# Hybrid SSD, attention and S5 trunk: the scan tables' powers, computed block by block among attention and the first output product

## The chip, the cores and the metric

The kernel runs on one core of one Trainium2 chip. The metric is the device time of one execution in microseconds; the median of the runs is compared. The engines are TensorE (PE in the profile; its weight loads are PEld), VectorE (DVE), ScalarE (ACT), GpSimd (POOL) and SyncE (SP), which issues most of the loads. DMAs are also issued by POOL.

## What is computed

A decoder trunk with two layers on 256 positions of width 2048, in float32. Layer 0 feeds one input projection to an SSD mixer and to causal attention, and maps both back by one output projection. Layer 1 is a diagonal complex state-space mixer (S5) with a gated product behind it. Cut to what matters here:

```python
def reference(x, ...):
    # layer 0
    z, xbc, dt, q, k, v, gate = split(x @ in0_w)
    xs, B, C = split(silu(causal_depthwise_conv(xbc)))
    y_a = rms_norm((ssd_scan(xs, dt, B, C) + d * xs) * silu(z))
    y_b = attention(rotary(q), rotary(k), v) * silu(gate)
    x = layer_norm(alpha * x + concat(y_a, y_b) @ out0_w)
    # layer 1
    u, gate = split(x @ in1_w)
    lam_bar = exp(lam * dt)                       # 128 groups x 64 complex states
    h_t = lam_bar * h_{t-1} + B_bar @ u_t         # per group of 16 channels
    y = gelu(Re(C @ h_t) + d * u)
    ga, gb = split(y @ glu_w)
    x = layer_norm(alpha * x + ((ga * sigmoid(gb)) * silu(gate)) @ out1_w)
```

## The kernel before

**Products.** All large products are done in float32 through pairs of a high and a low part. A unit of work is 256 rows by 512 columns of a weight: SP loads it (`raw`, L221), ScalarE takes the high part (`wh`, L224), VectorE the low part (`wl`, L226), and TensorE runs three matmuls for each tile (L277 with the weight as the stationary operand, L264 with the activation). Weights are split three units ahead, in rings of four buffers. A product has 8 units (16 in the first output product), and the products follow one another without a pause: two for B and C, four for the convolved x, four for z, then for each of four groups of heads q, k, v and gate, then four output products of 16 units, and then layer 1.

**Side work.** Everything else is written as small jobs which are put between the units. `jobs` holds the jobs that must be done within the next product; `pump` takes them evenly over its units. `back` holds slower work that is spread over many units, up to a unit given by `goal`. The order in which instructions stand on each engine is not the written order: a planner simulates the engines with costs of its own, and on each engine puts next what is ready by its own due times, the earliest written first. It fixes that order before the run. Each engine then works through its queue in order.

**The S5 tables.** `trig_job` and `table_job` compute `phi` (a complex number of modulus 1 for each of 64 columns), `rho` and others from the parameters, on VectorE and ScalarE, while the first convolved product runs. From these come the tables of sixteen blocks, which go to memory as `wb[b]` (128 x 1792) and are loaded in layer 1 (`load`, the tile `wt`):

- `phasor_job` computes, on POOL, the powers 0 to 63 of `phi` by doubling, cosines and sines in `cs`, with the products in `pq`: two memsets (L603, L604), two copies (L606), then six steps of two multiplies (L611), a subtraction (L613) and an addition (L614), and the DMAs to columns 1280 to 1791 of `wb` (L617). One job serves two blocks, on 8 columns of `phi`. `cs` and `pq` lie in the big buffer F behind `cbm`, whose place the attention output takes later. Two such jobs are put into `jobs` behind each of the four convolved products.
- `block_jobs(b)` computes the rest of block b: `bars` and `efs` on VectorE (`bb`, `et`, `tm`, and `ob`, which L663 begins), `pes` with transposes on TensorE and a copy on ScalarE (L678) and the store of `ob` on POOL (L685), and for each second block `mts` with the store of `om` (L698). `ob` has two buffers. These jobs go into `back` within the first group of heads, with a goal at the end of the third output product.

**The scan's sum of squares.** The SSD scan runs as `head_jobs` out of `back`, from the first z product to the first v product. For each two of its sixteen steps `comb` squares a result on ScalarE (L779) into a tile of the tag `c2` (three buffers of 2 KB a partition), and POOL adds it to `ssq` (L781).

**Other work on POOL.** The rotary add of q and k (L832) for every group of heads. Once layer 0 is written, its pools of buffers are released, and the rows of the layer norm are loaded by SP into that memory (L977).

The functions that the diff touches:

Of the kernel before, what the change touches and what calls it, by code (L numbers as in the profile page):

```python
# [12 lines left out]
OP = mybir.AluOpType  # L13
# [3 lines left out]
P = 128  # L17
# [141 lines left out]
def trunk(tc, io, out):  # L159
    nc = tc.nc  # L160
    V, A, G, T = nc.vector, nc.scalar, nc.gpsimd, nc.tensor
    count = [0]

    def nm(s):
        count[0] += 1
        return f"{s}_{count[0]}"

    with ExitStack() as top:
# [23 lines left out]
        def big(tag, shape, dt=F32):  # L192
            return slot.tile(shape, dt, tag=tag, name=nm(tag))
# [36 lines left out]
        jobs = deque()  # L230
        back = deque()
# [18 lines left out]
        def finish():  # L250
            while back:
                back.popleft()()
            goal[1] = 0.0
# [27 lines left out]
        def product(kind, hl, nu=CU, prelude=None):  # L281
            ps = banks()
            for u in range(nu):
                if prelude:
                    prelude(u)
                split_to(unit[0] + 3)
                wpair = ready.pop(unit[0])
                if kind == "w":
                    wmm(ps, u, nu, hl, wpair)
                else:  # L290
                    last = u == nu - 1
                    steps = [(j, o) for o in range(2) for j in range(UK)] if last else [(j, o) for j in range(UK) for o in range(2)]
                    for j, o in steps:
                        xmm(ps, o, wpair, j, hl(u * UK + j), u == 0 and j == 0, last and j == UK - 1)
                unit[0] += 1
                pump(nu - 1 - u)
            return ps
# [55 lines left out]
        wb = [dram.tile([P, 1792], F32, name=f"wb{b}") for b in range(16)]  # L353
# [9 lines left out]
        with ExitStack() as l0:  # L363
# [3 lines left out]
            def a4(shape, dt=F32):  # L367
                return wk.tile(shape, dt, tag="a4", bufs=6, name=nm("a4"))
# [4 lines left out]
            def c2(shape):  # L373
                return wk.tile(shape, F32, tag="c2", bufs=3, name=nm("c2"))
# [130 lines left out]
            conv_jobs(ps, 4, cT)  # L505
            fmem = big("F", [P, 4096])
            cbm = fmem[:, 0:1536].rearrange("p (g n) -> p g n", g=4)
            cs = fmem[:, 1536:2560].rearrange("p (a q c) -> p a q c", a=2, q=8)
            pq = fmem[:, 2560:3584].rearrange("p (i a q c) -> p i a q c", i=2, a=2, q=8)

            def cb_job(g):
                def go():
                    px = aux()
                    T.matmul(px[:, 0:256], bT[:, g, 0:P], cT[:, g, :], start=True, stop=True)
                    T.matmul(px[:, 256:384], bT[:, g, P:S], cT[:, g, P:S], start=True, stop=True)
                    V.tensor_tensor(cbm[:, g, 0:128], px[:, 0:128], C("tril"), op=OP.mult)
                    A.activation(cbm[:, g, 128:256], px[:, 128:256], AF.Copy)
                    V.tensor_tensor(cbm[:, g, 256:384], px[:, 256:384], C("tril"), op=OP.mult)
                return go
# [77 lines left out]
                        V.tensor_tensor(tq, ai, br, op=OP.mult)  # L597
                        V.tensor_tensor(w[:, 1, :, k], tp, tq, op=OP.add)

            def phasor_job(k):  # L600
                def go():
                    sl = slice(8 * k, 8 * k + 8)
                    G.memset(cs[:, 0, :, 0:1], 1.0)  # L603
                    G.memset(cs[:, 1, :, 0:1], 0.0)  # L604
                    for i in range(2):
                        G.tensor_copy(cs[:, i, :, 1], phi[:, i, sl])  # L606
                    n = 1
                    while n < 64:
                        m = min(n, 63 - n)
                        for i in range(2):  # L610
                            G.tensor_tensor(pq[:, i, :, :, 0:m], cs[:, :, :, 1 : m + 1],  # L611
                                            cs[:, i, :, n : n + 1].unsqueeze(1).to_broadcast([P, 2, 8, m]), op=OP.mult)
                        G.tensor_tensor(cs[:, 0, :, n + 1 : n + 1 + m], pq[:, 0, 0, :, 0:m], pq[:, 1, 1, :, 0:m], op=OP.subtract)  # L613
                        G.tensor_tensor(cs[:, 1, :, n + 1 : n + 1 + m], pq[:, 0, 1, :, 0:m], pq[:, 1, 0, :, 0:m], op=OP.add)  # L614
                        n *= 2
                    for i in range(2):
                        nc.gpsimd.dma_start(wb[2 * k + i][:, 1280:1792].rearrange("p (a n) -> p a n", a=2),  # L617
                                            cs[:, :, 4 * i : 4 * i + 4, :].rearrange("p a q c -> p a (q c)"))
                return go

            ktp = [None]
# [85 lines left out]
            def xs_jobs(ps, j):  # L707
                xT = a4([P, 4, S])
                conv_jobs(ps, 8 + 4 * j, xT)

                def back(t):
                    def go():
                        px = aux()
                        transpose4(px, [xT[:, f, t * P : t * P + P] for f in range(4)])
                        A.activation(xs[:, t, 512 * j : 512 * j + 512], px, AF.Copy)
                    return go

                while held:
                    jobs.append(held.popleft())
                held.extend([back(0), back(1)])  # L720

            for j in range(4):
                ps = product("w", xhl)
                xs_jobs(ps, j)
                jobs.extend([phasor_job(2 * j), phasor_job(2 * j + 1)])

            sz = big("D", [P, KT, S])
            ssq = wk.tile([P, S], F32, name="ssq")
# [73 lines left out]
            def scale_job(f):  # L802
                def go():
                    for ft in (f, f + 1):
                        V.scalar_tensor_tensor(sz[:, ft, :], sz[:, ft, :], PR("normg")[:, ft : ft + 1], ssq, op0=OP.mult, op1=OP.mult)
                return go
# [15 lines left out]
            def rope_jobs(ps, dst):  # L822
                def rot(i):
                    def go():
                        pv = ps[i].rearrange("p (f n) -> p f n", n=S)
                        q = dst[:, 2 * i : 2 * i + 2, :]
                        tm = b3([64, 2, S])
                        A.activation(q[64:128], pv[64:128], AF.Copy)
                        V.tensor_tensor(q[0:64], pv[0:64], cosb, op=OP.mult)
                        V.tensor_tensor(tm[0:32], pv[32:64], sinb[32:64], op=OP.mult)  # L830
                        V.tensor_tensor(tm[32:64], pv[0:32], sinb[0:32], op=OP.mult)
                        G.tensor_tensor(q[0:64], q[0:64], tm, op=OP.add)  # L832
                    return go

                jobs.extend([rot(0), rot(1)])
# [61 lines left out]
            for g in range(4):  # L897
                ps = product("w", xhl)
                qT = a4([P, 4, S])
                rope_jobs(ps, qT)  # L900
                ps = product("w", xhl)
                kT = a4([P, 4, S])
                rope_jobs(ps, kT)
                ps = product("x", xhl)
                v = a4([P, 2, 512])
                jobs.extend([lambda ps=ps, v=v, t=t: A.activation(v[:, t, :], ps[t], AF.Copy) for t in range(2)])
                if g == 0:
                    finish()
                    back.append(rms_job)
                    back.extend([scale_job(2 * f) for f in range(8)])  # L910
                    for b in range(16):
                        back.extend(block_jobs(b))
                    goal[0] = unit[0] + 13 * CU + 6 * CU
                ps = product("w", xhl)
                sg = a4([P, 4, S])
                jobs.extend([lambda ps=ps, sg=sg, i=i: A.activation(sg[:, 2 * i : 2 * i + 2, :].rearrange("p f n -> p (f n)"), ps[i], AF.Silu)
                             for i in range(2)])
                attn_jobs(g, qT, kT, v, sg)
# [364 lines left out]
```

## Time and profile before

| | us |
|---|---|
| median of 3 runs (1377.31 to 1377.97) | 1377.62 |
| the profiled execution, whole | 1377.72 |
| its span in the profile | 1375.6 |
| TensorE busy | 1356.2 |
| VectorE busy | 981.8 |
| ScalarE busy | 679.5 |
| POOL busy | 306.2 |

A row of a group of instructions reads: line, engine, operation, written tile <- read tiles with the shape, count | busy us, mean ns of one | idle time of the engine just before them and what ended it. In a row of the timeline the first number is the start, the second the length, and a bracket gives the idle time before it and the releaser. A row of the waits gives the total, the number and the longest. Stretches give the busy time of the engines, then TensorE's granted clock, the DMA share and GB/s.

### The profile page before, as it was taken

Reading aid. Unit: us, or ns where it says so; the run is one execution under the profiler, and the core shown is the slowest. Engines: PE = TensorE matmul, PEld = TensorE weight load, DVE = VectorE, ACT = ScalarE, POOL = GpSimd, SP = SyncE. Lnnn points to the kernel's source line nnn. Section 1 sums busy time; section 2 is a strip of 40 time slices with the busy share of each in tenths; the row PEclk is TensorE's granted clock in tenths of the full one; section 3 lists DMA queues with packets and bytes.
Section 4 is the critical chain, followed back from the end, with each engine's and each line's share of the span. In section 5 each row is a group of like instructions: output and inputs, shape, how many; then the busy total and the mean of one; then the engine's idle time right before and its main releaser. Section 6 shows DMA issues by size and latency. Waiting matters only on the chain.

```text
span 1375.6 us, 27155 instructions
## 1 busy us (share of the span) xinstructions
PE 1356.2 (99%) x11064; PEld 1273.4 (93%) x11064; DVE 981.8 (71%) x1556; ACT 679.5 (49%) x872; POOL 306.2 (22%) x457
## 2 busy tenths in 40 slices
PE   9999999999999999999999999999999999999996
PEld 9999999988998998998988888899999999999885
DVE  5789958777767688687768756758788846454556
ACT  5565468765544544554554435244345545444441
POOL 0258776842011011011000000023433100000001
PEclk9999999999999999999999999999999999999998
DMA  8546665445556656657656669488888665555762
GB/s 306 176 150 190 211 203 189 159 149 192 171 158 201 205 177 210 213 165 228 221 184 222 224 211 323 159 254 275 283 275 277 197 203 183 182 182 182 253 208 86
DMA packets 79212, 283.14 MB, mean 206 GB/s; under 512 B 9840, under 2 KB 10480, under 8 KB 78576
## 3 DMA queue, kind: packets, MB, share of 16 engines
q1 hardware_dynamic: 68112, 239.33, 53.8%
q0 software_dynamic: 10400, 40.90, 9.1%
q8 instruction: 86, 1.41, 0.4%
q10 hardware_dynamic: 576, 1.18, 0.2%
q14 instruction: 38, 0.31, 0.1%
HBM read 260.41 MB, written 20.97 MB: 205 GB/s over the span
## 4 chain that ended last, share of the span: by engine, by line
PE 82%; POOL 10%; DMA 3%; DVE 2%; issue 1%; ACT 1%; POOLq 0%; SPq 0%; ACTq 0%
PE main L277 50%; PE main L264 26%; POOL F L611 5%; DMA wb<-F 2%; POOL F L613 2%; POOL F L614 2%; POOL F L606 1%; PE enc L1093 1%; PE aux L677 1%; PE aux L341 1%; PE aux L349 1%; PE dec L1138 1%; PE aux L673 1%; PE aux L851 1%; PE aux L883 1%
## 5 line engine op out<-in xcount | busy, mean ns | idle before, releaser
L226 DVE TENSOR_TENSOR wl<-raw,wh 128x1024 fp32r<-128x1024 f32 x431 | 538.9, 1255 | 281.9 <-ACT wh L224 275.7
L224 ACT ACTIVATE wh<-raw 128x1024 fp32r<-128x1024 f32 x431 | 454.7, 1058 | 535.8 <-PE main L277 325.5
L277 PE MATMUL main<-A,wl 128*128 128x256 f32 x1920 | 545.5, 284 | 3.7 <-DVE wl L226 3.6
L277 PE MATMUL main<-A,wh 128*128 128x256 f32 x1920 | 548.4, 286 | 0.0
L277 PE MATMUL main<-B,wh 128*128 128x256 f32 x1920 | 544.4, 284 | 0.0
L277 PEld LDWEIGHTS main<-A,wl 128*128 128x128 f32 x1920 | 369.0, 192 | 4.6 <-DVE wl L226 4.5
L277 PEld LDWEIGHTS main<-A,wh 128*128 128x128 f32 x1920 | 369.2, 192 | 0.8 <-issue 0.2
L277 PEld LDWEIGHTS main<-B,wh 128*128 128x128 f32 x1920 | 369.3, 192 | 0.3
L277 PE MATMUL main<-C,wh 128*128 128x256 f32 x512 | 148.1, 291 | 0.7 <-ACT C L1004 0.7
L277 PE MATMUL main<-F,wh 128*128 128x256 f32 x512 | 145.4, 285 | 0.1
L277 PE MATMUL main<-C,wl 128*128 128x256 f32 x512 | 145.1, 284 | 0.0
L277 PEld LDWEIGHTS main<-C,wh 128*128 128x128 f32 x512 | 98.3, 192 | 2.9 <-ACT C L1004 0.9
L264 PE MATMUL main<-wh,A 128*128 128x512 f32 x256 | 100.7, 393 | 0.0
L264 PE MATMUL main<-wl,A 128*128 128x512 f32 x256 | 100.1, 391 | 0.0
L264 PE MATMUL main<-wh,C 128*128 128x512 f32 x256 | 100.0, 392 | 0.0
L264 PE MATMUL main<-wh,B 128*128 128x512 f32 x256 | 99.9, 390 | 0.0
L264 PE MATMUL main<-wl,C 128*128 128x512 f32 x256 | 99.8, 390 | 0.0
L264 PE MATMUL main<-wh,F 128*128 128x512 f32 x256 | 99.8, 390 | 0.0
L277 PEld LDWEIGHTS main<-F,wh 128*128 128x128 f32 x512 | 98.7, 193 | 0.4 <-DVE F L1005 0.4
L277 PEld LDWEIGHTS main<-C,wl 128*128 128x128 f32 x512 | 98.7, 193 | 0.1
L611 POOL TENSOR_TENSOR F<-F 128x16 f32<-128x16 f32 (+5 forms) x96 | 67.1, 720 | 3.8
L685 POOL DMA_DIRECT2D wb<-ob x16 | 8.8, 547 | 254.2 <-ACT ob L678 200.3
(279 smaller groups left out, 1565.2 us busy)
## 6 DMA issues: line engine op xcount, KB each, us to landing
raw<-in_wi SPq DMA_DIRECT2D x271, 512.0 KB, 4.2
raw<-in_wo SPq DMA_DIRECT2D x96, 512.0 KB, 4.2
raw<-in_wglu SPq DMA_DIRECT2D x64, 512.0 KB, 3.5
wt<-wb POOLq DMA_DIRECT2D x16, 896.0 KB, 7.6
wb<-ob POOLq DMA_DIRECT2D x16, 512.0 KB, 4.4
bc<-in_s5bc SPq DMA_DIRECT2D x16, 256.0 KB, 4.4
wb<-F POOLq DMA_DIRECT2D x16, 256.0 KB, 3.8
wb<-om POOLq DMA_DIRECT2D x16, 128.0 KB, 4.2
```

Source lines behind the costliest of these rows:

```text
L224: last["a"] = A.activation(wh, raw, AF.Copy)
L226: last["v"] = V.tensor_tensor(wl, raw, wh.bitcast(F32), op=OP.subtract)
L264: T.matmul(ps[o], l[:, k, sl], r[:, j, :], start=start and i == 0, stop=stop and i == 2)
L277: T.matmul(pv[o // 2][:, o % 2, :], l[:, j, sl], r[:, k, :], start=first and i == 0 and o % 2 == 0, stop=end and i == 2 and o % 2 == 1, sk ...
L341: T.transpose(dst[:, i * P : i * P + P], s, ident)
L349: T.matmul(px[:64, 0:64], idle, idle, start=i == 0, stop=i == n - 1)
L606: G.tensor_copy(cs[:, i, :, 1], phi[:, i, sl])
L611: G.tensor_tensor(pq[:, i, :, :, 0:m], cs[:, :, :, 1 : m + 1], cs[:, i, :, n : n + 1].unsqueeze(1).to_broadcast([P, 2, 8, m]), op=OP.mult)
L613: G.tensor_tensor(cs[:, 0, :, n + 1 : n + 1 + m], pq[:, 0, 0, :, 0:m], pq[:, 1, 1, :, 0:m], op=OP.subtract)
L614: G.tensor_tensor(cs[:, 1, :, n + 1 : n + 1 + m], pq[:, 0, 1, :, 0:m], pq[:, 1, 0, :, 0:m], op=OP.add)
L673: T.transpose(pe[:, a * P : a * P + P], ev[:, a, :], ident)
L677: T.matmul(pk[at : at + 64, a * 16 : a * 16 + 16], ev[:, a, 64 * i : 64 * i + 64], cv[:, a, i, :], start=True, stop=True)
```

## The change

Each block gets a powers job of its own, on 4 columns of `phi` instead of 8, with one DMA instead of two. Its three tiles (`cs`, `p0`, `p1`) come from the tag `c2` and no longer lie in F. The job is put into `back`, behind the jobs of its block, and no longer into `jobs` behind the convolved products. The columns, the doubling steps and what is written to `wb` stay the same.

```diff
-            cs = fmem[:, 1536:2560].rearrange("p (a q c) -> p a q c", a=2, q=8)
-            pq = fmem[:, 2560:3584].rearrange("p (i a q c) -> p i a q c", i=2, a=2, q=8)
...
-            def phasor_job(k):
+            def phasor_job(b):
                 def go():
-                    sl = slice(8 * k, 8 * k + 8)
+                    sl = slice(4 * b, 4 * b + 4)
+                    cs, p0, p1 = (c2([P, 2, 4, 64]) for _ in range(3))
+                    pq = (p0, p1)
...
                         for i in range(2):
-                            G.tensor_tensor(pq[:, i, :, :, 0:m], cs[:, :, :, 1 : m + 1],
-                                            cs[:, i, :, n : n + 1].unsqueeze(1).to_broadcast([P, 2, 8, m]), op=OP.mult)
-                        G.tensor_tensor(cs[:, 0, :, n + 1 : n + 1 + m], pq[:, 0, 0, :, 0:m], pq[:, 1, 1, :, 0:m], op=OP.subtract)
-                        G.tensor_tensor(cs[:, 1, :, n + 1 : n + 1 + m], pq[:, 0, 1, :, 0:m], pq[:, 1, 0, :, 0:m], op=OP.add)
+                            G.tensor_tensor(pq[i][:, :, :, 0:m], cs[:, :, :, 1 : m + 1],
+                                            cs[:, i, :, n : n + 1].unsqueeze(1).to_broadcast([P, 2, 4, m]), op=OP.mult)
+                        G.tensor_tensor(cs[:, 0, :, n + 1 : n + 1 + m], p0[:, 0, :, 0:m], p1[:, 1, :, 0:m], op=OP.subtract)
+                        G.tensor_tensor(cs[:, 1, :, n + 1 : n + 1 + m], p0[:, 1, :, 0:m], p1[:, 0, :, 0:m], op=OP.add)
                         n *= 2
-                    for i in range(2):
-                        nc.gpsimd.dma_start(wb[2 * k + i][:, 1280:1792].rearrange("p (a n) -> p a n", a=2),
-                                            cs[:, :, 4 * i : 4 * i + 4, :].rearrange("p a q c -> p a (q c)"))
+                    nc.gpsimd.dma_start(wb[b][:, 1280:1792].rearrange("p (a n) -> p a n", a=2), cs.rearrange("p a q c -> p a (q c)"))
...
             for j in range(4):
                 ps = product("w", xhl)
                 xs_jobs(ps, j)
-                jobs.extend([phasor_job(2 * j), phasor_job(2 * j + 1)])
...
                     for b in range(16):
-                        back.extend(block_jobs(b))
+                        back.extend(block_jobs(b) + [phasor_job(b)])
```

## The prediction

> **What bounds the kernel now.** I read the page first, then stretches of 40 us, then the waits behind the gaps.
>
> ```profile
> span 1375.6 us, 27155 instructions
> ...
> PE 1356.2 (99%) x11064; PEld 1273.4 (93%) x11064; DVE 981.8 (71%) x1556; ACT 679.5 (49%) x872; POOL 306.2 (22%) x457
> ...
> PE 82%; POOL 10%; DMA 3%; DVE 2%; issue 1%; ACT 1%; POOLq 0%; SPq 0%; ACTq 0%
> ```
>
> TensorE is busy for 1356.2 of 1375.6 us, so at most 19.4 us can be won, while a new wait of TensorE counts in full. Yet POOL has 10% of the chain that ended last. The stretches (PE, PEld, DVE, ACT, POOL busy, then clock and DMA) show where POOL touches TensorE:
>
> ```profile
> 130.00:170.00 40.00, 38.35 (x316) 37.74 (x316) 37.85 (x67) 19.77 (x26) 32.29 (x47) 1.00 0.63 200
> 250.00:290.00 40.00, 37.99 (x316) 35.62 (x315) 27.99 (x41) 26.70 (x39) 29.60 (x44) 1.00 0.48 156
> 530.00:570.00 40.00, 40.00 (x293) 36.80 (x292) 29.41 (x59) 17.28 (x21) 4.49 (x5) 1.00 0.69 225
> ```
>
> While POOL computes the powers (it is busy 32.29 and 29.60 of 40 us), TensorE loses 40 - 38.35 = 1.65 us and 40 - 37.99 = 2.01 us. In the attention, at 530 us, it loses nothing and POOL is almost idle. Stretches of 5 us of TensorE alone narrow the gaps down, and the queue of ScalarE and the chain name the cause of the second:
>
> ```profile
> 140.00:145.00 5.00, 3.57 (x28) 1.00 0.42 143
> 285.00:290.00 5.00, 2.99 (x26) 1.00 0.34 103
> ```
>
> ```profile
> 280.07 0.63 ACT L779 ACTIVATE c<-D 128x512 f32<-128x512 f32 x1 [7.54 <-POOL ssq L781]
> ```
>
> ```profile
> 276.49 0.67 POOL F L614
> 277.16 0.68 POOL ssq L781
> ```
>
> The fourth Square of the scan (L779, tag c2, three buffers) needs a buffer which POOL's sum of squares (L781) frees, and that stands behind the last powers job. ScalarE is held for 7.54 us, its weight splits come late, and TensorE stands for 2.01 us. So TensorE rides over 7.54 - 2.01 = 5.5 us of a late split.
>
> **What the change removes.** With the powers out of POOL's queue before 280 us, the sum of squares runs when its Square is done, and the 2.01 us go. The 1.65 us at 143 us fall where VectorE is busy 37.85 of 40 us; its own weight split is slower while POOL works. In order: 90 to 280 us, 300 to 690, 690 to 860:
>
> ```profile
> L226 DVE TENSOR_TENSOR wl<-raw,wh 128x1024 fp32r<-128x1024 f32 x58 | 78.8, 1362 | 13.2 <-ACT wh L224 13.2
> L226 DVE TENSOR_TENSOR wl<-raw,wh 128x1024 fp32r<-128x1024 f32 x124 | 156.0, 1266 | 54.9 <-ACT wh L224 54.4
> L226 DVE TENSOR_TENSOR wl<-raw,wh 128x1024 fp32r<-128x1024 f32 x60 | 72.9, 1222 | 40.7 <-ACT wh L224 40.3
> ```
>
> At 1222 instead of 1362 ns VectorE has 10% of room there, enough for 1.65 us. Gain: between 2.0 and 3.7 us, taken at 3.7, since both gaps have POOL beside them. The same slowing moves to the attention: 7.6% on 1266 ns (to 1362) takes 29.41 to some 31.6 of 40 us. That leaves room; I take nothing, with 1.65 us as the upper bound, one gap like that at 143 us.
>
> [...]
>
> **What it adds: POOL's work.** Each block now has its own chain of 24 multiplies and adds and 2 copies, on 4 columns instead of 8; the DMAs stay 16, of 256 KB.
>
> ```profile
> L611 POOL TENSOR_TENSOR F<-F 128x16 f32<-128x16 f32 (+5 forms) x96 | 67.1, 720 | 3.8
> L613 POOL TENSOR_TENSOR F<-F 128x8 f32<-128x8 f32 (+5 forms) x48 | 28.6, 596 | 3.8
> L614 POOL TENSOR_TENSOR F<-F 128x8 f32<-128x8 f32 (+5 forms) x48 | 24.4, 508 | 0.0
> L617 POOL DMA_DIRECT2D wb<-F x16 | 12.0, 754 | 2.1 <-POOL F L614 2.1
> L606 POOL COPY F<-phi 128x8 f32<-128x8 f32 x16 | 11.8, 766 | 15.6 <-DVE phi L557 8.2 <-DVE phi L556 7.1 <-issue 0.3
> ```
>
> ```profile
> L611 POOL TENSOR_TENSOR F<-F 128x496 f32<-128x496 f32 x16 | 21.9, 1390 | 0.6
> L611 POOL TENSOR_TENSOR F<-F 128x16 f32<-128x16 f32 x16 | 5.0, 334 | 0.7
> ```
>
> ```profile
> POOL F L603 <- DMA wb<-F: 29.0, 7, 5.3
> DVE tm L636 <- DMA bc<-in_s5bc: 26.3, 12, 3.0
> ```
>
> Halving the columns shifts every size by one class: of L611's 67.1 us the largest form (21.9) drops out and the smallest (5.0) is there twice: 50.2, a factor of 0.75. On all three lines: 0.75 x (67.1 + 28.6 + 24.4) = 90 us for eight chains, 180 us for sixteen. With copies (2 x 11.8) and issues (12.0) it is 216 us, 13.5 us a block. Each next chain reuses a buffer that the last one's DMA still reads: 29.0 / 7 = 4.1 us of waiting each time now, so up to 17.6 us a block.
>
> [...]
>
> **When it runs.** Each engine's queue is ordered ahead of time, and work is put far ahead of where it is written:
>
> ```profile
> 1.31 0.11 POOL L603 MEMSET F<- 128x8 f32 x1
> ```
>
> ```profile
> 142.91 0.41 DVE L663 TENSOR_TENSOR ob<-bc,lap 128x256 f32<-128x256 f32 x1
> ```
>
> The memset that begins the powers is written behind the first convolution product and ran at 1.31 us. A block job (L663), written inside the attention, ran at 142.91 us. A block's powers need nothing but phi and buffers, so I expect them not one by one among the attention's jobs, but packed into POOL's queue as soon as buffers allow. The buffers are the three of c2, behind the eight Squares; the last sum of squares ends at 334.96 + 1.73 = 336.7 us:
>
> ```profile
> 334.96 1.73 POOL L781 TENSOR_TENSOR ssq<-ssq,c 128x256 f32<-128x256 f32 x2 [6.06 <-ACT c L779]
> 433.53 0.57 POOL L685 DMA_DIRECT2D wb<-ob  x1 [5.95 <-ACT ob L678]
> 537.11 0.56 POOL L685 DMA_DIRECT2D wb<-ob  x1 [4.32 <-ACT ob L678]
> ```
>
> ```profile
> 443.11 0.42 DVE L663 TENSOR_TENSOR ob<-bc,lap 128x256 f32<-128x256 f32 x1
> 547.29 0.41 DVE L663 TENSOR_TENSOR ob<-bc,lap 128x256 f32<-128x256 f32 x1
> ```
>
> ```profile
> wb<-ob POOLq DMA_DIRECT2D x16, 512.0 KB, 4.4
> ```
>
> So POOL is full from 336.7 to 336.7 + 16 x 17.6 = 618 us, as long as the attention. In that queue also stand the rotary adds (L832) and the stores of finished blocks (L685). A store's place is fixed by the pace that the planner gives POOL; if the chip is slower, the store comes late. Who waits: block b+2 writes the same buffer ob (two of them) on VectorE at L663, in VectorE's queue ahead of weight splits, hence TensorE. Today the slack is 443.11 - (433.53 + 4.4) = 5.2 us for block 0 and 547.29 - (537.11 + 4.4) = 5.8 us for block 4. With the 5.5 us that TensorE rides over, a lag of 10.7 and 11.3 us is free; every further microsecond stops TensorE.
>
> The lag per block is what the trace does not show. Lower bound 0: the planner's pace is right. Upper bound 4.1: the whole DMA wait is unplanned. The nearest row is L636, a reader of another DMA, queued 26.3 / 12 = 2.2 us too early on average; I take 2.0. Then a block is planned at 15.6 us: by block 0's store (433.5 - 336.7) / 15.6 = 6.2 blocks, 12.4 us of lag, 1.7 over the free amount; by block 4's store (537.1 - 336.7) / 15.6 = 12.8 blocks, 25.7 us, 14.4 over. Overruns don't add up, as each stop lets POOL catch up; the largest counts. While VectorE stands, POOL's operations are faster, for which I take off 2.4: 12 us.
>
> **Sum.** The profiled execution took 1377.7 us (span 1375.6 and 2.1 around it), 0.1 above the median of 1377.62: 1377.7 - 3.7 + 12 = **1386 us**. At a lag of 0.9 or less nothing exceeds the free amount: 1374. At 4.1 a block is planned at 13.5, block 4's store has 14.8 x 4.1 = 61 us of lag, 49.5 over: 1423.5.
>
> **Rivals.**
> First, not slower: POOL keeps its places. It decides at a lag of 0.95 us a block (11.3 / 12). For it: the planner may price POOL's operations generously, and small ones are what the change doubles. Against: the 2.2 us of L636 and the 7.54 us of L779, both places where a queue was ordered for a release that came later. Time: 1377.7 - 3.7 = 1374.0, with the 1.65 us of contention up to 1375.7.
>
> Second: no packing; the powers run where they are written, one block every (537.1 - 433.5) / 4 = 26 us, with no lag. Then the last one stands behind the last block's store, and the row loads on SP, with weight loads behind them, wait for the release of that memory:
>
> ```profile
> 818.64 1.08 POOL L698 DMA_DIRECT2D wb<-om  x2 [6.42 <-ACT om L696]
> ```
>
> ```profile
> 823.46 0.80 SPq L977 DMA_DIRECT2D row<-in_lnr  x2
> ```
>
> ```profile
> 833.35 1.06 ACT L224 ACTIVATE wh<-raw 128x1024 fp32r<-128x1024 f32 x1 [4.16 <-DMA raw<-in_wo]
> ```
>
> The last powers would end at 819.7 + 13.5 = 833.2 and land 4.1 later, at 837.3, instead of 823.46: 13.8 us, of which 5.5 - 4.16 = 1.3 are free. Time: 1374.0 + 12.5 = 1386.5. Against it is the memset at 1.31 us.
>
> Third, the change doesn't do what it says: the chains are packed ahead of the scan's Squares, from 97 us on as now, and nothing moves: 1377.7. Against: three buffers, shared with those Squares.
>
> **Chances and range.** Lag 0.58, POOL on time 0.27, no packing 0.10, nothing moves 0.05. Of the first, 0.05 ends within 0.2% (2.75 us, about what a measurement of this kernel can tell from no change); of the second, 0.20 is faster by more and 0.07 within. Faster 0.20, same 0.05 + 0.07 + 0.05 = 0.17, slower 0.53 + 0.10 = 0.63. The lag case alone goes from 1377 to 1410 (a lag of 3.2: 14.4 planned, 13.9 blocks, 44.5 us, 33 over, 1407). The range takes in POOL on time: 1373 to 1410.
>
> **What the profile after would show.** POOL idle between 97 and 220 us, L226 near 1250 ns there, and no gaps at 143 and 287 us: the gain. The powers from about 337 us on, back to back: the packing. VectorE's L663 waiting for the DMA wb<-ob between 440 and 600 us, with gaps of TensorE behind it: the lag. No such wait and a full TensorE would be the first rival. Powers up to 833 us and a late row load would be the second. I am wrong if TensorE's new gaps stand elsewhere, at the scores behind L832 for one.

## The result: slower by 2.5%, and the profile after

The median went from 1377.46 us (the three runs listed above and one more, 1377.25 to 1377.97) to 1412.57 us (four runs, 1409.04 to 1416.33): a ratio of 1.0252, interval 1.0237 to 1.0267. The forecast was 1386 us. The profiled execution after took 1415.96 us, its span 1414.2, which is 38.6 us more than the span before; it is 3.4 us above the median, and what follows is read from that execution. First the lines of the page that answer to those of before:

```profile
span 1414.2 us, 27370 instructions
...
PE 1362.6 (96%) x11064; PEld 1279.6 (90%) x11064; DVE 966.8 (68%) x1556; ACT 684.3 (48%) x874; POOL 343.6 (24%) x681
...
PE 81%; POOL 13%; DMA 4%; issue 2%; DVE 1%; ACT 0%; POOLq 0%; DVEq 0%
```

TensorE is busy for 1362.6 us, 6.4 more than before for the same 11064 matmuls, and POOL has 13% of the chain that ended last. The stretches of 40 us (busy time of PE, PEld, DVE, ACT, POOL, then the clock granted to TensorE, DMA share, GB/s) show where the span grew:

```profile
130.00:170.00 40.00, 40.00 (x338) 40.00 (x335) 30.34 (x58) 22.32 (x27) 0.00 (x0) 1.00 0.59 182
250.00:290.00 40.00, 40.00 (x336) 38.00 (x332) 27.25 (x42) 31.23 (x48) 5.98 (x7) 1.00 0.51 158
410.00:450.00 40.00, 29.09 (x177) 24.36 (x175) 21.92 (x35) 14.11 (x17) 31.30 (x84) 0.90 0.41 138
450.00:490.00 40.00, 36.45 (x295) 35.95 (x296) 30.62 (x61) 16.59 (x22) 34.72 (x70) 0.93 0.64 211
490.00:530.00 40.00, 24.91 (x194) 24.23 (x193) 19.85 (x48) 13.27 (x26) 29.98 (x88) 0.79 0.37 125
530.00:570.00 40.00, 40.00 (x282) 36.95 (x281) 34.68 (x58) 17.10 (x21) 34.71 (x71) 1.00 0.58 185
570.00:610.00 40.00, 33.18 (x248) 31.76 (x247) 22.12 (x42) 15.12 (x19) 11.51 (x23) 0.91 0.64 211
```

Both old gaps are gone: TensorE is full at 130 and at 250 us. From 410 to 610 us it now idles for 10.91 + 3.55 + 15.09 + 6.82 = 36.4 us. With the 6.4 us of slower matmuls behind those stops, and less the 1.65 and 2.01 us won, that is 39.1 us, against 38.6 measured.

Who is late is read from four queues. First POOL's timeline: the start of the first powers chain, the first and the last of the sixteen stores of powers (L615), and the stores of `ob` (L682) of blocks 0 and 4:

```profile
321.75 0.10 POOL L602 MEMSET c<- 128x4 f32 x1
...
342.55 0.77 POOL L615 DMA_DIRECT2D wb<-c  x1 [0.31 <-POOL c L613]
...
445.16 0.58 POOL L682 DMA_DIRECT2D wb<-ob  x1
...
577.16 0.58 POOL L615 DMA_DIRECT2D wb<-c  x1 [0.30 <-POOL c L613]
...
578.97 0.55 POOL L682 DMA_DIRECT2D wb<-ob  x1
```

Then ScalarE's copies that complete the `ob` of blocks 0 and 4, VectorE's three longest waits (for the stores of blocks 0, 2 and 4), and TensorE's two longest:

```profile
412.94 0.60 ACT L675 ACTIVATE ob<-aux 128x512 f32<-128x512 f32 x1
...
554.15 0.60 ACT L675 ACTIVATE ob<-aux 128x512 f32<-128x512 f32 x1
```

```profile
448.13 2.03 DVE L660 TENSOR_TENSOR ob<-bc,lap 128x256 f32<-128x256 f32 x2 [13.82 <-DMA wb<-ob]
...
505.05 0.51 DVE L660 TENSOR_TENSOR ob<-bc,lap 128x256 f32<-128x256 f32 x1 [13.75 <-DMA wb<-ob]
...
581.89 0.76 DVE L660 TENSOR_TENSOR ob<-bc,lap 128x256 f32<-128x256 f32 x2 [7.10 <-DMA wb<-ob]
```

```profile
451.74 1.65 PE L689 MATMUL aux<-kt,consts 128*128 128x128 f32 x6 [12.64 <-DVE kt L681]
...
508.83 0.44 PE L341 MATMUL aux<-consts,b 128*128 128x128 f32 x1 [15.09 <-DVE b L865]
```

The chains run packed from 321.75 to 577.16 us, one in (577.16 - 342.55) / 15 = 15.6 us. Block 0's `ob` is complete at 413.54 us, but its store stands behind more than seven chains and is issued at 445.16: 31.6 us late, counted from the end of the copy. VectorE's write of the same buffer for block 2 (L660, before L663) stands for 13.82 us, and with it what is queued behind it on VectorE: `kt` (L681), the attention's `b` (L865), and weight splits. TensorE's queue holds matmuls that read `kt` and `b`, so it stops for 12.64 and 15.09 us. The waits give the totals:

```profile
DVE ob L660 <- DMA wb<-ob: 38.1, 5, 13.8
POOL c L610 <- DMA wb<-c: 29.1, 13, 4.8
```

Five waits of 38.1 us on VectorE stand against 36.4 us on TensorE.

### The profile page after: what moved, and what is told of

It reads as the page before. It is cut to its first block, busy times and chain, and to the rows that moved or that the text cites. A ratio compares the mean times of both kernels' runs of the same rounds, so it can differ in the third digit from the quotient of the medians.

```text
span 1414.2 us, 27370 instructions
## 1 busy us (share of the span) xinstructions
PE 1362.6 (96%) x11064; PEld 1279.6 (90%) x11064; DVE 966.8 (68%) x1556; ACT 684.3 (48%) x874; POOL 343.6 (24%) x681
## 4 chain that ended last, share of the span: by engine, by line
PE 81%; POOL 13%; DMA 4%; issue 2%; DVE 1%; ACT 0%; POOLq 0%; DVEq 0%
PE main L277 53%; PE main L264 21%; POOL c L610 6%; DMA wb<-c 4%; POOL c L612 3%; POOL c L613 2%; PE enc L1089 1%; PE aux L341 1%; PE aux L767 1%; PE aux L349 1%; PE dec L1134 1%; PE aux L737 0%; PE dec L1130 0%; PE aux L674 0%; POOL a L828 0%
## 5 line engine op out<-in xcount | busy, mean ns | idle before, releaser
L610 POOL TENSOR_TENSOR c<-c 128x8 f32<-128x8 f32 (+2 forms) x192 | 89.0, 481 | 36.6 <-DMA wb<-c 29.1
L777 POOL TENSOR_TENSOR ssq<-ssq,c 128x256 f32<-128x256 f32 x16 | 13.0, 815 | 217.2 <-ACT c L775 216.5
```

The source lines that it names most:

```text
L610: G.tensor_tensor(pq[i][:, :, :, 0:m], cs[:, :, :, 1 : m + 1], cs[:, i, :, n : n + 1].unsqueeze(1).to_broadcast([P, 2, 4, m]), op=OP.mult)
```

## The experiments

The theory: powers chains that run ahead hold up, in POOL's queue, work with readers (block 0's store by 31.6 us), and nothing else of the change costs time. The rivals: the chains cost by slowing VectorE's weight splits or through their DMAs; the new place as such; one shared buffer alone.

**One store out of the queue.** In the changed kernel the store of `ob` is issued by ScalarE.

```diff
-                    nc.gpsimd.dma_start(wb[b][:, 0:1024], ob)
+                    nc.scalar.dma_start(wb[b][:, 0:1024], ob)
```

> The changed kernel, but the finished block's ob is stored from ScalarE's queue instead of POOL's; the powers stay packed in POOL's queue. Theory (POOL runs behind its planned places, the store of ob comes late behind the powers, VectorE waits at L660 for its buffer): the 38 us of waits at L660 go, TensorE has no gap between 430 and 590 us, 1374 to 1376 us. [...] Rival 2 (the rotary adds late behind the powers hold the scores): they still stand in POOL's queue, 1390 us or more.

1389.27 us (1386.31 to 1401.01; before 1378.05), ratio 1.0070, interval 1.0047 to 1.0094. It missed 1374 to 1376. The waits of the profiled execution, the slowest of its runs:

```profile
DVE om L691 <- DMA wb<-om: 27.6, 2, 25.5
ACT om L693 <- DMA wb<-om: 24.4, 1, 24.4
PE main L277 <- DVE wl L226: 23.4, 2, 22.4
```

No wait for `wb<-ob` is left; the other store in POOL's queue, that of `om` with its one buffer, has taken its place. The median lies next to the 1390 us of rival 2, but TensorE has no wait for a rotary add in this execution. The mechanism stood, the list of what it holds was too short.

**A third buffer for half of it.** VectorE's half of `ob` gets a tile of its own (`of`, three buffers) and a store of its own.

```diff
-                    ob = h["ob"] = pp.tile([P, 1024], F32, tag="ob", bufs=2, name=nm("ob"))
+                    of = h["of"] = pp.tile([P, 512], F32, tag="of", bufs=3, name=nm("of"))
```

> The changed kernel, but ob is two tiles: the part that VectorE begins with L660 has three buffers instead of two, the part from TensorE two, each with a store of its own (16 DMA issues more on POOL). Theory: VectorE's reader comes one block later, some 20 to 26 us more slack than the 5 to 10 us of before; a lag of 2.2 us a block (35 us after sixteen) is covered but for a few us: 1374 to 1385 us. [...]

1385.15 us (one execution), just above what was expected. VectorE's wait is gone, and ScalarE's copy and `om` wait instead:

```profile
ACT ob L676 <- DMA wb<-ob: 14.6, 2, 11.2
DVE om L693 <- DMA wb<-om: 10.9, 1, 10.9
```

A buffer more moves the stop and shortens it (7.74 us of TensorE from 530 to 570 us), but doesn't end it.

**The DMA wait inside the chains.** The tag `c2` gets four buffers.

```diff
-                return wk.tile(shape, F32, tag="c2", bufs=3, name=nm("c2"))
+                return wk.tile(shape, F32, tag="c2", bufs=4, name=nm("c2"))
```

> The changed kernel with four buffers for the tag c2 instead of three, so a chain of powers need not wait for the DMA of the one before (29 us in all, 13 waits). If the lag is that wait, which the planner counted shorter: no lag, 1374 to 1380 us. If the planner prices POOL's operations themselves too low: the lag per block stays near 2 us, the waits at L660 stay near 30 us or more, 1400 us or more.

1408.47 us (one execution). The chains now wait 2.4 us for their DMAs instead of 29.1, and yet:

```profile
POOL c L602 <- DMA wb<-c: 2.4, 2, 1.9
...
DVE ob L660 <- DMA wb<-ob: 28.8, 3, 15.4
```

TensorE still loses 10.05 + 3.01 + 14.69 + 0.87 = 28.6 us from 410 to 570 us. With the DMA waits gone, about 8 of the 36.4 us go, and the rest stays. Block 0's store is still 30.6 us late (445.00 against 414.40), now behind 8.5 chains: 3.6 us a chain, almost without a DMA wait. The order was planned anew for four buffers, so the 8 us are the difference of two kernels and not the price of the wait alone.

**Each chain behind its own block's store.** A planner's constraint keeps the chain of block b behind the store of block b on POOL.

```diff
-                    nc.gpsimd.dma_start(wb[b][:, 0:1024], ob)
+                    h["st"] = stores[b] = nc.gpsimd.dma_start(wb[b][:, 0:1024], ob)
...
+                    with tc.issue_after(stores[b].ins):
+                        powers(b)
```

> The changed kernel, but on POOL each block's powers are held behind that block's own store, so that they no longer stand packed ahead of the stores. Theory: POOL has one chain (15 us) for each 26 us, no lag builds up, no wait at L660, both gaps of the kernel before are gone: 1374 to 1376 us. Rival (the last chain behind the last store holds the row loads, the second rival of the prediction): no gaps before 800 us, one of some 12 us at 835 us, 1386 us.

1376.22 us (1373.82 to 1377.98; before 1378.05), ratio 0.9984, interval 0.9974 to 0.9993; 0.2 us above what was expected. Same chains, same buffers, and the loss is gone. Block 0's `ob` and its store:

```profile
413.32 0.60 ACT L682 ACTIVATE ob<-aux 128x512 f32<-128x512 f32 x1
```

```profile
414.22 0.77 POOL L689 DMA_DIRECT2D wb<-ob  x1 [13.44 <-ACT ob L682]
```

The store is issued 0.3 us after its data, and POOL waits for it. So the chains cost nothing when they stand behind the stores. But they are also no longer packed here: the last one issues its store at 819.73 us instead of 577.16, so order and density changed together, and this run alone can't tell them apart.

**Both stores out of the queue.** As in the first experiment, and `wb<-om` too from ScalarE.

```diff
-                        nc.gpsimd.dma_start(wb[b - 1 + i][:, 1024:1280], om[:, 256 * i : 256 * i + 256])
+                        nc.scalar.dma_start(wb[b - 1 + i][:, 1024:1280], om[:, 256 * i : 256 * i + 256])
```

> Both stores that stand in POOL's queue behind the power chains, wb<-ob and wb<-om, are issued from ScalarE's queue; the chains stay packed as in the changed kernel. Theory (late stores are the whole route from the late chains to TensorE): no wait of ob on DMA wb<-ob or of om on DMA wb<-om over 5 us, TensorE idle under 3 us between 410 and 610 us, 1374 to 1379 us. [...] Rival B (the lag moves on a third time, to the chains' own last stores and the row loads behind them near 690 us): 1379 to 1395 us, with the loss after 610 us.

1385.52 us (1383.95 to 1386.60; before 1377.22), ratio 1.0056, interval 1.0043 to 1.0069. The stores' waits are gone, and TensorE has one stop; its row, and POOL's:

```profile
585.68 0.80 PE L846 MATMUL aux<-a,a 128*128 128x128 f32 x2 [10.57 <-POOL a L828]
```

```profile
583.75 0.58 POOL L615 DMA_DIRECT2D wb<-c  x1 [0.30 <-POOL c L613]
584.35 2.49 POOL L828 TENSOR_TENSOR a<-a,b 64x512 f32<-64x512 f32 x2
```

The rotary add (L828, before L832) runs only when the last chain has issued its store, and the attention scores (L846) wait for it. The 10.57 us lost are a wait for POOL's add, not for slowed splits. "The late stores are the whole route" is wrong: it is everything with a reader in that queue. This is the place that the prediction named last, under what would make it wrong.

**The pin, with both stores at ScalarE.**

```diff
-                    nc.gpsimd.dma_start(wb[b][:, 0:1024], ob)
+                    h["st"] = stores[b] = nc.scalar.dma_start(wb[b][:, 0:1024], ob)
```

> Each block's chain is kept behind its own store, as in the kernel pinned before, and both stores are issued from ScalarE's queue besides. Theory: with the pin POOL's queue holds no store up, so moving the stores brings nothing more than the 1.3 us that TensorE still idled between 450 and 490 us: 1374 to 1376.5, a ratio to the kernel before of 0.997 to 0.999. Rival (the stores' wait in POOL's queue still costs with the pin): 1372 or less. Rival (the issues cost ScalarE its splits): above 1378.

1384.81 us (1383.10 to 1393.12; before 1377.22), ratio 1.0065, interval 1.0043 to 1.0087: a miss. POOL is busy for 33.0 us from 330 to 370 us, against 1.3 with the pin alone: a constraint on a store in another queue did not hold the chains back on POOL. It is the kernel above once more, and again the scores wait for the rotary add (6.9 us). That wait, not splits held up by ScalarE's issues, is why the time lies above 1378.

**Every second chain pinned.**

```diff
+                    if b % 2:
+                        with tc.issue_after(stores[b].ins):
+                            powers(b)
+                    else:
+                        powers(b)
```

> Only the odd blocks' chains are kept behind their own block's store; the eight even ones stay free and may be packed ahead as in the changed kernel. Theory (the loss is the sum of what each chain run ahead is late, about 2.15 us, less some 2.7 us that are free): 8 x 2.15 - 2.7 = 14.5 us and 2 or 3 us of lower clock, on 1374: about 1391, between 1384 and 1397. Rival (what my prediction assumed, only the largest overrun counts against a free 10.7 us): 8 x 2.0 - 10.7 = 5 us or less, 1376 to 1380. Rival (all or nothing: any packing brings the whole loss): 1405 or above.

1377.09 us (one execution). It settles nothing about the dose, though it lies in the first rival's range: the chains share three buffers in turn, so a free chain stays behind the pinned one before it. POOL is busy for only 12.8 and 4.0 us in the two stretches from 330 to 410 us; nothing was packed.

**The first eight chains free, the last eight pinned.**

```diff
+                    if b >= 8:
+                        with tc.issue_after(stores[b].ins):
+                            powers(b)
+                    else:
+                        powers(b)
```

> The chains of blocks 0 to 7 stay free and are packed from 322 us on as in the changed kernel; those of blocks 8 to 15 are kept behind their own block's store. Theory (lateness grows by 2.1 to 2.2 us with each chain run ahead, and each stall is paid in full): the first eight chains bring the changed kernel's first two stalls, 10.9 and 3.6 us of TensorE, and 2 to 3 us of lower clock, on 1376; the later two, 15.1 and 6.8 us, are gone: 1389 to 1395 us. Rival (a first stall puts all later blocks behind, whatever the later chains do): 1403 or above. Rival (the planner sets the free chains otherwise as soon as the later ones are held, as with every second chain held): under 1380 us.

1384.55 us (1383.49 to 1385.78; before 1378.68), ratio 1.0046, interval 1.0029 to 1.0063. VectorE has one such wait left, and TensorE one stop of 10.5 us:

```profile
DVE ob L670 <- DMA wb<-ob: 10.8, 1, 10.8
PE aux L699 <- DVE kt L691: 10.5, 1, 10.5
```

The later stops are gone, as the theory has it, but the second of the first two is gone too, and the figure expected was 5 us too high. Its 2.1 to 2.2 us a chain rested on an error of mine: I had paired the store at 445.16 us with the copy of block 1 (428.65) instead of block 0 (413.54). Rightly paired, lateness is 31.6 us there; here the store of block 0 is 29.5 us late (443.46 against 413.95), and VectorE waits for 10.8 of them.

**Back at the old place.** The small chains in the three buffers stand behind the convolved products again, four behind each.

```diff
+                jobs.extend([phasor_job(4 * j + i) for i in range(4)])
...
-                        back.extend(block_jobs(b) + [phasor_job(b)])
+                        back.extend(block_jobs(b))
```

> The four-column chains in the three rotating buffers are put back at the old place, four after each convolution product; nothing else of the change is undone. Theory (the place is not what costs; chains that POOL does slower than the order was made for hold whatever shares their queue or buffers): sixteen chains of 13.5 us and 4.1 us of DMA wait, 282 us, start near 65 us and end near 345, some 55 us past where the old ones ended; the Squares of attention and POOL's sums of them, which share the three buffers and the queue, are held from 287 us on, TensorE idles 15 us or more there, 1395 to 1440 us. Rival (the place among attention and the first output product is what costs): within 5 us of the kernel before, 1373 to 1383.

1413.34 us (one execution), inside 1395 to 1440. TensorE stops at 285 us, not in the attention:

```profile
ACT c L776 <- POOL c L613: 46.2, 1, 46.2
PE main L277 <- ACT wh L224: 36.2, 1, 36.2
```

Here the Squares (L776 in this kernel) share the three buffers with the chains, and ScalarE holds its weight splits behind them. The loss doesn't need the new place; chains stop whoever waits behind them for a buffer or in the queue.

**POOL's queue cleared, chains still packed.** Both stores from ScalarE, and the rotary add on VectorE.

```diff
-                        G.tensor_tensor(q[0:64], q[0:64], tm, op=OP.add)
+                        V.tensor_tensor(q[0:64], q[0:64], tm, op=OP.add)
```

> The chains stay packed on POOL, and everything of the attention stage that stood behind them in POOL's queue and has a reader is taken out of it: both stores (wb<-ob, wb<-om) are issued from ScalarE's queue, and the rotation's add a<-a,b is done on VectorE. Theory (the whole loss is work held in POOL's in-order queue behind late chains): TensorE idle under 4 us between 300 and 690 us, 1374 to 1379 us. Rival A (the lag finds a fourth reader): again one idle stretch of 5 us or more before 690 us, 1380 to 1390. Rival B (VectorE has no room for sixteen more adds of 0.7 us and is slowed by POOL besides): losses of 1 to 2 us spread over the stage behind wl L226, 1380 to 1388, with no long stretch.

1374.73 us (1372.20 to 1376.88; before 1378.68), ratio 0.9971, interval 0.9962 to 0.9981: 0.3% faster than the kernel before. The stretches of this kernel:

```profile
450.00:490.00 40.00, 38.84 (x325) 37.96 (x323) 31.79 (x69) 21.05 (x36) 33.40 (x73) 1.00 0.64 216
490.00:530.00 40.00, 40.00 (x322) 38.12 (x321) 36.12 (x61) 18.68 (x24) 35.19 (x81) 1.00 0.62 198
530.00:570.00 40.00, 40.00 (x291) 37.32 (x290) 29.78 (x56) 17.21 (x20) 36.60 (x78) 1.00 0.72 227
```

POOL is as full as in the changed kernel (35.19 and 36.60 of 40 us), and TensorE loses 1.16 us between 290 and 690 us. With the queue held free of readers, packed chains cost next to nothing. Together with the pinned kernel, which left the readers in the queue and moved the chains, this settles the route: readers behind late chains. What it rules out is a cost of the chains through VectorE's splits beyond that 1.16 us; what the splits do to POOL's own pace is another matter, and the last section returns to it.

**Where the gain comes from.** The same three moves in the kernel before, and the kernel above again, on one chip.

> The kernel before, with the powers at their old place, and with the same three moves as in the kernel whose POOL queue was cleared (both stores issued from ScalarE's queue, the rotation's add on VectorE). Theory (the gain of 4 us of that kernel comes from taking the powers out of the convolution stage; the three moves alone bring nothing): 1376 to 1379.5 us, the two idle stretches at 143 and 287 us still there. Rival (the three moves are what gains, wherever the powers are): 1373 to 1375.5.

> The changed kernel with its POOL queue cleared (both stores issued from ScalarE's queue, the rotation's add on VectorE), once more, beside the kernel before with the same moves. Theory: 1373 to 1376 us, a ratio to the kernel before of 0.996 to 0.998. Rival (the first measurement was a lucky one): within 0.2% of the kernel before.

The kernel before with the moves: 1376.94 us (1373.57 to 1379.88; before 1377.67), ratio 0.9996, interval 0.9987 to 1.0004. TensorE still loses 1.69 and 1.99 us at the two old gaps (busy 38.31 and 38.01 of 40). The cleared kernel again: 1374.88 us (1372.52 to 1377.84), ratio 0.9974, interval 0.9963 to 0.9985. The moves alone bring nothing that can be measured, and moving the powers brings 2.1 us beside them, 2.8 to 4.0 us against the kernel before.

## Why the prediction was wrong

**The gain, 3.7 us: right.** Both gaps closed, and the experiments put the gain at 2.1 to 4.0 us. VectorE's weight split in the changed kernel, from 90 to 280 and from 300 to 690 us:

```profile
L226 DVE TENSOR_TENSOR wl<-raw,wh 128x1024 fp32r<-128x1024 f32 x61 | 74.4, 1222 | 24.8 <-ACT wh L224 24.5
L226 DVE TENSOR_TENSOR wl<-raw,wh 128x1024 fp32r<-128x1024 f32 x110 | 140.8, 1290 | 47.5 <-ACT wh L224 47.1
```

1362 went to 1222 ns, and where the powers are now, 1266 to 1290 (the forecast let it go to 1362). Taking nothing for VectorE was right within 1.2 us, as the cleared kernel shows. The prediction looked at POOL's side only for the time in which VectorE stands (the 2.4 us below).

**The packing: right.** Chains back to back as soon as the Squares' buffers allow, from 321.75 instead of 336.7 us (the last sum of squares runs inside the first chain), at 15.6 instead of 17.6 us each: the DMA wait was 29.1 / 16 = 1.8 us, not 4.1. POOL's work was put too high, not too low: its multiplies and adds took 167.4 us, not 180, its copies 12.4 instead of 23.6.

**The route: right, but not whole.** Late store, L663, VectorE, TensorE came as forecast. The store of `om` and the rotary add stand behind it on the same route; the experiments met them one after the other.

**The lag, 2.0 us a block: wrong, and this is the step that failed.** Block 0's store was 31.6 us late after 7.4 chains, 4.3 us a chain, just past the upper bound of 4.1 (which stood for another cause, the DMA wait). For block 4, the lateness is 578.97 - 554.75 = 24.2 us, behind stops that had already moved everything else by 10.91 + 3.55 + 15.09 = 29.6: 53.8 us after sixteen chains, 3.4 each. The forecast had 12.8 chains and 25.7 us. (Part of this can be slack that the planner itself left; the traces don't show its plan.) The nearest row that I chose, L636 with 2.2 us, is a wait for a DMA and says nothing of POOL's pace. What the runs show instead is 3.4 to 4.3 us a chain, the size of what VectorE's weight splits cost POOL's operations (last section). The bound's own time was 1423.5 us; the range stopped at a lag of 3.2, 1407 by its sum, at 1410, and so left the result out. The 2.4 us taken off for POOL running faster while VectorE stands were my estimate, and no run shows that figure; what the runs show is a chain of 9.1 us while VectorE stood still, against 13.0 us beside a working VectorE (last section), and such a gain is already inside the lateness measured here.

**The free amount, 10.7 and 11.3 us: too low at both blocks.** Free is the lateness that VectorE didn't wait for. At block 0 it is 31.6 - 13.82 = 17.8 us, at block 4 it is 24.2 - 7.10 = 17.1. It isn't one number, though: at block 2, which the prediction didn't look at, the store was 24.0 us late (502.09 against 478.06) and VectorE waited for 13.75 of them, so only 10.3 were free. The 5.5 us that TensorE was to ride over don't exist here: it lost 12.64 of VectorE's first 13.82, since it waits for `kt` and `b` directly and not only for splits.

**"The largest counts": right, as an account.** 53.8 - 17.8 = 36.0 us, against 36.4 measured. Most of that agreement is built in: 29.6 us of both sides are the same three stops, and only the last stop is compared, 24.2 - 17.8 = 6.4 against 6.82. A freer test is the kernel with eight chains: its lateness less the free amount of the changed kernel is 29.5 - 17.8 = 11.7, against a stop of 10.5.

**The clock: left out.** The 6.4 us of slower matmuls had no term. With it and the measured lag: 1377.7 - 3.7 + 36.0 + 6.4 = 1416.4, against 1415.96; this adds up what one execution shows and forecasts nothing. The first rival, 1374.0, is about what the cleared kernel reaches (1374.73): its condition, POOL on time, can be had in another way, by leaving nothing behind POOL. The second and the third rival didn't occur. The pinned kernel comes near the second, with a chain behind each block's store, and doesn't pay the 12.5 us forecast for it: the last store of powers is issued at 819.73 us and the row loads run at 823.74, against 823.46 in the kernel before.

## What to carry to other kernels

Before work is moved to an engine that looks idle, list everything else in that engine's queue that has a reader (stores, buffer releases, small operations of other stages): here, long free-running work was put ahead of it and held it up by the accumulated error in pace, and the stops came to about the largest lateness less the slack where the reader stands (36.0 us by that account, 36.4 measured). Either tie the moved work behind what is urgent in the same queue, or take the urgent work out of that queue; a buffer more, or one store less, only handed the wait on (waits of up to 11.2 and 25.5 us in the new places). When lateness is read from a trace, pair each store with its own block by counting from the first.

## What the runs showed of the hardware

**A POOL operation that began during one of VectorE's weight splits ended only after the split.** In the kernel with the chains at the old place, VectorE stood still from 285 to 320 us; there three chains ran alone. One of them, with its beginning, its wait for a DMA, two of its operations and the beginning of the next:

```profile
288.42 0.12 POOL L602 MEMSET c<- 128x4 f32 x1
...
290.20 0.21 POOL L610 TENSOR_TENSOR c<-c 128x8 f32<-128x8 f32 x1 [1.09 <-DMA wb<-c]
...
290.93 0.39 POOL L610 TENSOR_TENSOR c<-c 128x16 f32<-128x16 f32 x2
...
295.58 1.18 POOL L610 TENSOR_TENSOR c<-c 128x248 f32<-128x248 f32 x2
...
298.57 0.12 POOL L602 MEMSET c<- 128x4 f32 x1
```

The same in the changed kernel, beside a working VectorE:

```profile
391.78 0.12 POOL L602 MEMSET c<- 128x4 f32 x1
...
396.09 0.21 POOL L610 TENSOR_TENSOR c<-c 128x8 f32<-128x8 f32 x1 [3.63 <-DMA wb<-c]
396.83 1.40 POOL L610 TENSOR_TENSOR c<-c 128x16 f32<-128x16 f32 x2
...
401.57 1.24 POOL L613 TENSOR_TENSOR c<-c,c 128x32 f32<-128x32 f32 x1
...
404.45 2.14 POOL L610 TENSOR_TENSOR c<-c 128x248 f32<-128x248 f32 x2
...
408.41 0.12 POOL L602 MEMSET c<- 128x4 f32 x1
```

Two of VectorE's weight splits in that time:

```profile
396.92 1.23 DVE L226 TENSOR_TENSOR wl<-raw,wh 128x1024 fp32r<-128x1024 f32 x1
...
401.48 1.23 DVE L226 TENSOR_TENSOR wl<-raw,wh 128x1024 fp32r<-128x1024 f32 x1 [1.65 <-ACT wh L224]
```

Without the DMA waits a chain takes 298.57 - 288.42 - 1.09 = 9.1 us alone and 408.41 - 391.78 - 3.63 = 13.0 us here: 3.9 us more. Four steps of the chain make up all of it; each overlaps a weight split of VectorE and grows by 0.9 to 1.0 us. The addition at 401.57, which takes 0.25 us alone, ends at 402.81, just after the split beside it (402.71). The split takes no longer than without POOL (1.22 us). Of the chains' 384 multiplies and adds, 47 began while a split ran: 46 of them ended 0.07 to 0.48 us after it, and 45 took 0.85 to 1.07 us longer than the shortest of their line and shape. Over all sixteen chains the multiplies and adds take 167.4 / 16 = 10.5 us a chain, against 7.3 alone. Counted operation by operation against the length alone, that is 53.2 us in all, 46.4 of them in operations that overlap a weight split. VectorE's products that read one operand from PSUM (L825 to L827) held nothing up: the 25 chain operations that ran beside these alone took at most 0.01 us longer.

That is about the size of the lag, 3.4 to 4.3 us a chain: 53.2 us by block 4's store, against a lateness of 53.8, though by block 0's only 22.9 of 31.6. That the planner reckons without this is likely, but was only argued: its costs aren't in the traces, and no run took this effect away and left the order. On VectorE's side the change cost 24 ns a split (1266 to 1290); the trace shows that POOL pays, with the 53.2 us above.

**The stops of TensorE cost more than their length.** Two stretches from the two longest stops, in the changed kernel:

```profile
440.00:450.00 10.00, 0.00 (x0) 0.00 (x0) 1.87 (x2) 0.67 (x2) 8.09 (x26) 0.59 0.19 79
500.00:510.00 10.00, 1.17 (x6) 1.20 (x7) 4.92 (x11) 1.93 (x5) 8.23 (x23) 0.50 0.33 118
```

The clock granted is 0.59 and 0.50, and the matmuls behind the stops run slower at first: 13 of them from 512 to 514 us, at a mean clock of 0.61, against 19 from 518 to 520 at 1.00. With the stop of 6.82 us that makes three such stretches; around the fourth stop, of 1.81 us, the clock stays at 1.00. In all TensorE is busy for 6.4 us more, on 36.4 of idling. The price did not grow with the length of a stop: the kernel with the chains at the old place has one stop of 36.2 us, and its span of 1411.5 us is 35.9 us longer than before, of which 34.7 us are more idling between 130 and 330 us (38.3 against 3.7); that leaves 1.2 us for slower matmuls.
